# Attention and residual blocks as parts of 8 KB tiles, experts' weights in twenty whole places

## The chip, the cores and the metric

The kernel runs on one core of one Trainium2 chip. The metric is the device time of one execution in microseconds (us). Engines are named as in the profile: PE is TensorE, DVE is VectorE, ACT is ScalarE, POOL is GpSimd, and SP is SyncE, which here issues nearly all DMAs. A tile has 128 partitions; sizes such as 8 KB are bytes of one partition, and 128 rows of 8 KB make 1 MB.

## The reference

```python
def reference(...):
    x = first_block(...)    # two layers: swiglu, three mixer branches (window attention,
                            # gated linear recurrence, attention to 256 memory rows), swiglu
    return second_block(x)  # one hybrid layer

def hybrid_layer(x, ...):   # 256 tokens, width 1024
    h = rms_norm(x, norm1_gain); p = h @ w_in
    y_att  = dilated_window_attention(...) @ w_att_out     # 3 groups x 4 heads
    y_rwkv = rwkv7_time_mix(...)                           # 8 heads
    x = x + (gates[..., :D] * y_att + gates[..., D:] * y_rwkv) @ w_out
    return x + hierarchical_moe(rms_norm(x, norm2_gain), ...)

def expert_block(xb, e):    # 32 experts (4 groups of 8), two of them per token
    hid = silu(xb @ w_expert_gate[e]) * (xb @ w_expert_up[e])    # 1024 -> 512
    return hid @ w_expert_down[e]                                # 512 -> 1024
```

All of it is float32. An expert's three matrices have 6 MB, the 32 experts 192 MB.

## The kernel before, in words

The first block and the hybrid layer's projections stream their weights through a ring of two 1 MB buffers (`raw`, class `Stream`, L121). Each half of a buffer is split by ACT (L126, `wh`) and DVE or POOL (L128, `wl`) into two parts, and PE takes three products (L144 to L146). In the hybrid layer three generators, attention, recurrence and gates, take turns by the string `ORDER`; then `hybrid_out` joins them, `route` picks the experts, and `moe` runs them.

`moe` takes the experts four at a time, in eight rounds. A round reads 24 units of 1 MB: eight of the gate matrices, eight of the up matrices (L1336, output `gu`) and eight of the down matrices (L1359, output `y`). A unit is one expert's share: four blocks k of 128x512. PE goes over the blocks k in the outer loop and over the four experts in the inner one, so that a unit's last block is used just before its group of four is done.

Where a unit is put is a list of places (`Units.at`), filled in turn: unit number i goes into place i mod 19. Places come free while the hybrid layer still runs: `free` adds them as its parts end (`LT`, `scores`, `RB`, `YZ`, `at`, `rw`), and `PACE` says after which of the last streamed weights more units are asked for. Some places are one tile of 8 KB. Others are put together from small tiles, four of 2 KB or two of 4 KB, because attention and the residual stream keep their values in 2 KB tiles: `qk` 6, `hv` 3, `bias` 3, `T` 3 (pools of `AB`) and `x` 6 (`NX`). Such a place is loaded by four DMAs with rows of 2 KB (L1129); POOL writes one element first where the load has to wait for a point in the program (L1113, L1121). The first place is loaded by four DMAs with rows of 2 KB on its second turn too. The last four units of the last round's up matrices, and the last four of its down matrices, are loaded in halves.

The DMAs of a queue start in the order in which SP issues them. A scheduler that runs at build time, with modelled times, sets this order; a DMA waits at SP for its tile's last reader. It also waits for one of eight completion counters, so that the ninth DMA is issued when the first has landed.

The residual stream `x` is written at L182 and L185 into a new `x` tile in each sublayer, in `hybrid_in` into new ones (`x1`), and in `hybrid_out` again (`x2`). After `moe` each engine reads a flag and branches over a block that is only for experts with more than 32 tokens; then the four output DMAs go (L1372).

Of the kernel before, what the change touches and what calls it, by code (L numbers as in the profile page):

```python
# [8 lines left out]
P=128  # L9
# [99 lines left out]
class Stream:  # L109
# [6 lines left out]
    def _load(s):  # L116
        c=s.c; nc=c.nc; i=s.pos
        if i and i%16==0:
            with c.tc.high_priority() if i>16 else ExitStack():
                s.raw=c.ring.tile([P,2048],F32,tag="ring",name="raw")  # L120
                nc.sync.dma_start(out=s.raw,in_=s.dram[i//16])  # L121
        if i%8==0:
            with c.tc.high_priority():
                s.wh=c.wsp.tile([P,1024],F32R,tag="wh",name="wh"); s.wl=c.wsp.tile([P,1024],F32R,tag="wl",name="wl")
                r=s.raw[:,(i%16)*128:(i%16)*128+1024]
                nc.scalar.copy(s.wh,r)  # L126
                e=nc.gpsimd if s.turns and s.turns[i//8%len(s.turns)] else nc.vector
                e.tensor_tensor(s.wl,r,s.wh.bitcast(F32),op=ALU.subtract)  # L128
            if s.reached: s.reached(s.wh)
# [4 lines left out]

W5=[P,512]
def pst(c,tag,name,shape=None): return c.where["p",tag].tile(shape or [P,2,256],F32,tag=tag,name=name,bufs=c.PT[tag])
def blk(c,tag,name,dt=F32,shape=None): return c.where["b",tag].tile(shape or [P,2,256],dt,tag=tag,name=name,bufs=c.BT[tag])
def bc(r,n=2): return r.unsqueeze(1).to_broadcast([P,n,256])
# [358 lines left out]
NX=6; NRING=2; NW=3  # L497

def pools(c,ex):
    tc=c.tc  # L500
    c.where={}; c.BT={}; c.PT={}
    c.kp=ex.enter_context(tc.tile_pool(name="kp",bufs=1))
    c.xp=ex.enter_context(tc.tile_pool(name="xp",bufs=NX))
    c.ring=ex.enter_context(tc.tile_pool(name="ring",bufs=NRING))
    c.dr=ex.enter_context(tc.tile_pool(name="dr",bufs=1,space=bass.MemoryType.DRAM))
# [18 lines left out]

def xblk(c,name="x"): return c.xp.tile([P,2,256],F32,tag="x",name=name)

# [76 lines left out]
ORDER='grrrggagargrgagaaggrgaagararggrrraarrragrragrrrrarrg'; NP=0; T1=(1, 1, 1, 0, 1, 1, 0, 1, 0); T2=(1, 0, 0, 1)  # L603
RB={"rw":20,"hc":1}; AB={"qk":6,"hv":3,"bias":3,"T":3}; HP={"r":3,"a":2}

# [66 lines left out]
def rwkv(c,X,Rb,lw,gu,gu2,ins):  # L672
# [195 lines left out]
    def advance(m):  # L868

        t=WC[m]; ps=pst(c,"r","st",[P,4,64])  # L870
        for i in range(4):
            for j in range(2):
                hf=slice(j*64,j*64+64); nc.tensor.matmul(ps[hf,i,:],t[hf,0,i,:],S[m][hf,i,:],start=True,stop=True)
        s=c.sm.tile([P,8,64],F32,tag="S",name="S",bufs=1)[:,:4]
        v.tensor_tensor(s,S[m],pe[:,m,:].unsqueeze(2).to_broadcast([P,4,64]),op=ALU.mult); v.tensor_tensor(t[:,1],t[:,1],s,op=ALU.add)
        v.tensor_tensor(t[:,1],t[:,1],ps,op=ALU.add)
        S.append(t[:,1])
# [45 lines left out]
def hyb_attention(c,X,Rb,rt,db):  # L923
# [38 lines left out]
    den=c.sm.tile([P,4,2,3],F32,tag="hden",name="hden",bufs=1); rd=c.sm.tile([P,4,2],F32,tag="hrd",name="hrd",bufs=1)  # L962
    oh,ol=[c.xp.tile([P,2,256],F32R,tag="x",name=n) for n in ("oh","ol")]
    yield
# [62 lines left out]
def hybrid_in(c,xs,ins,att,rwk):  # L1027
# [5 lines left out]
    for p in range(4):  # L1033
        t=xblk(c,"x1")
        for i in range(2): v.scalar_tensor_tensor(t[:,i,:],xs[p][:,i,:],gf[:,2*p+i:2*p+i+1],Rf,op0=ALU.mult,op1=ALU.mult)
        x1.append(t)
# [11 lines left out]
def hybrid_out(c,xs):  # L1048
# [13 lines left out]
    for p in range(4):  # L1062
        ps=w[2*p:2*p+2] if p<2 else gemm_last(c,8,M,"wo") if p==3 else gemm_pair(c,8,M,"wo")
        t=xblk(c,"x2"); add_out(c,t,ps,x1[p],None); yield t

MP={"y":2,"a":3}
NRW=5
PACE=[0, 0, 0, 0, 1, 2, 0, 0, 0, 0, 0, 0, 1, 1, 1, 0, 0, 1, 0, 0, 0, 3, 1, 0]
# [19 lines left out]
def moe_consts(c,ins):  # L1088
# [3 lines left out]
    c.mc=c.kp.tile([P,136+CAP],F32,name="mc"); nc.sync.dma_start(out=c.mc,in_=ins['mc'])  # L1092

class Units:

    def __init__(s,c,ex,ins): c.un=s; s.c=c; s.ex=ex; s.ins=ins; s.i=0; s.got=[]; s.two=[]; s.at=[]; s.j=0; s.big=None; s.gap=[]
    def pool(s,name,bufs=1): return s.ex.enter_context(s.c.tc.tile_pool(name=name,bufs=bufs,reuse_waits="tile")),"u"
# [3 lines left out]
    def load(s,after=None):  # L1101

        c=s.c; nc=c.nc; i=s.i; s.i+=1; n=s.j%len(s.at); p=s.at[n]; again=s.j//len(s.at)==1; s.j+=1
        w=s.ins['we'][i//24,i%24//8,i%8//4,i%4]; last=i>=176 and i%8>3; Q=range(0,2048,512)
        back=range(4)[::-1] if n<2 else range(4)
        def tile(x,n):
            b=1 if x[1]=="S" else c.BT.get(x[1])
            return x[0].tile([P,n],F32,tag=x[1],name="unit",**({"bufs":b} if b else {}))
        with c.tc.high_priority():
            if len(p)==1 and not (again and n==0):  # L1110
                r=tile(p[0],2048); q=[r[:,a:a+512] for a in Q]
                if n==0: s.big=q
                if after is not None: nc.gpsimd.tensor_copy(r[:1,:1],after[:1,:1].bitcast(F32))  # L1113
                z=[[(r[:,a],w[:,a])] for a in (slice(0,1024),slice(1024,2048))] if last else [[(r,w)]]
            else:

                if len(p)==1: q=s.big
                elif len(p)==2: q=[t[:,a:a+512] for t in [tile(x,1024) for x in p] for a in (0,512)]
                else: q=[tile(x,512) for x in p]
                if after is not None:  # L1120
                    for t in q: nc.gpsimd.tensor_copy(t[:1,:1],after[:1,:1].bitcast(F32))  # L1121
                z=[[(q[k],w[:,k*512:k*512+512])] for k in back]
            if last:

                s.two.append([sum(z[:len(z)//2],[]),sum(z[len(z)//2:],[])])
                z=[sum(x,[]) for x in zip(*s.two)] if i%4==3 else []
                if i%4==3: s.two=[]
            for x in z:
                for d,src in x: nc.sync.dma_start(out=d,in_=src)  # L1129
        return q  # L1130
# [3 lines left out]
    def free(s,name):  # L1134

        c=s.c; A=lambda t,n: [(c.where["b",t],t)]*n
        if name=="LT": s.more((c.u8,"big"))
        if name=="scores": s.more(*A("qk",4)); s.more(*A("qk",2),*A("bias",2))
        if name in ("RB","YZ"): s.more((c.r8,"u"))
        if name=="at": s.more(*A("hv",3),*A("bias",1)); s.gap.append(0)  # L1140
        if name=="rw":
            s.rest=[s.pool(f"u{i}") for i in range(NRW)]+[s.pool("gap",2)]; s.gap.append(0)
        if len(s.gap)==2:

            g=s.rest.pop(); s.gap=[]
# [124 lines left out]
def moe(c,m,ins,out):  # L1270
    nc=c.nc; v=nc.vector
    q=m.q; G5=m.G5; rt=m.rt; g32=vec(c,'norm2'); io=m.io; acc=m.acc; Hh=m.Hh; Hl=m.Hl; mt=m
    def overflow(acc):
        over=nc.values_load(mt.fi,min_val=0,max_val=1)
        with c.tc.If(over>0):
            x=[t[:,2*i:2*i+2,:] for t in [c.wsp.tile([P,4,256],F32,tag=n,name="ox") for n in ("wh","wl")] for i in range(2)]
            for t in range(2):
                for n in range(2):
                    w=xblk(c,"oh").rearrange("p a b -> p (a b)")
                    for p in range(2): v.tensor_tensor(w[:,p*256:p*256+256],Hh[2*n+p][:,t,:].bitcast(F32),Hl[2*n+p][:,t,:].bitcast(F32),op=ALU.add)  # L1280
# [5 lines left out]
            with c.tc.For_i(0,8,1) as r:  # L1286
                ge=c.sm.tile([P,2,1,4],F32,tag="oge",name="oge",bufs=1)
                nc.sync.dma_start(out=ge,in_=mt.dG[:,:,bass.ds(r,1),:])
                for e in range(4):
# [94 lines left out]
def body(tc,v,ins,out,dbg=None):  # L1384
    with ExitStack() as ex:
# [34 lines left out]
```

## Time and profile before

| | |
|---|---|
| three runs, median | 2137.96 us (2134.9 to 2139.03) |
| the profiled execution, its own time | 2128.82 us |
| its span | 2127.1 us |
| PE busy | 1946.0 us (91%) |
| DVE, ACT, POOL busy | 1139.9, 842.4, 94.0 us |
| first expert matmul `gu` starts | 1654.5 us |
| moved by DMA in all | 475.27 MB |

The span is one execution's from its first to its last instruction; its own time is 1.7 us longer. Instruction counts are the profile's: a float32 matmul stands there twice.

### The profile page before, as it was taken

To read this page: it belongs to the slowest core of one execution; us is meant where nothing else is said; L and a number is where in the kernel's file an instruction comes from. 1 tells how busy PE (TensorE), PEld (TensorE's weight loads), DVE (VectorE), ACT (ScalarE), POOL (GpSimd) and SP (SyncE) were. 2 spreads that over 40 slices of the span, in tenths; PEclk is the share of its full clock that TensorE was granted. 3 is DMA by queue.
4 is the path that set the end of the run, shared out by engine and by line. 5 is a ranking of instruction groups with operands and counts; after the bars stand their busy time and mean duration, and the time that the engine had idled before them with its cause. 6 is when DMAs were issued, how large, how long until landed. Compare 5 with 4: busy or idle time off the path is not lost.

```text
span 2127.1 us, 35735 instructions
## 1 busy us (share of the span) xinstructions
PE 1946.0 (91%) x15063; PEld 1668.7 (78%) x15063; DVE 1139.9 (54%) x1778; ACT 842.4 (40%) x1253; POOL 94.0 (4%) x71
## 2 busy tenths in 40 slices
PE   8999999999999999999998999999998876767665
PEld 8999999999999999999997999898988321212111
DVE  6566786676656566687575656776667210101110
ACT  5454565444444444476544444543534100000000
POOL 0000000000000000000000000444002000000000
PEclk9999999999999999999999999999999898888788
DMA  6565444455555555534457555433549899999997
GB/s 210 181 226 185 162 139 139 171 186 179 178 181 183 188 201 200 180 138 141 159 181 181 179 180 186 166 120 100 184 140 355 333 397 410 398 404 401 395 405 297
DMA packets 109617, 475.27 MB, mean 223 GB/s; under 512 B 17737, under 2 KB 21356, under 8 KB 63372
## 3 DMA queue, kind: packets, MB, share of 16 engines
q1 hardware_dynamic: 96624, 462.07, 59.8%
q10 hardware_dynamic: 12828, 10.87, 2.2%
q8 instruction: 120, 1.97, 0.4%
q14 instruction: 45, 0.37, 0.0%
HBM read 468.93 MB, written 3.96 MB: 222 GB/s over the span
## 4 chain that ended last, share of the span: by engine, by line
PE 73%; DMA 21%; DVE 4%; ACT 1%; issue 0%; SPq 0%; POOL 0%; ACTq 0%; DVEq 0%
DMA unit<-in_we 19%; PE g L144 4%; PE g L145 4%; PE g L146 4%; PE d L145 4%; PE d L144 4%; PE d L146 4%; PE u L146 4%; PE u L144 4%; PE u L145 4%; PE gt L144 3%; PE gt L146 3%; PE gt L145 3%; DMA raw<-in_w 2%; PE br L145 2%; PE br L146 2%
## 5 line engine op out<-in xcount | busy, mean ns | idle before, releaser
L126 ACT CAST wh<-raw 128x1024 fp32r<-128x1024 f32 x491 | 513.8, 1048 | 692.3 <-PE g L145 128.9
L128 DVE TENSOR_TENSOR wl<-raw,wh 128x1024 fp32r<-128x1024 f32 x469 | 575.4, 1227 | 341.8 <-ACT wh L126 338.1
L1336 PE MATMUL gu<-unit,W 128*32 128x512 f32 x1024 | 185.9, 735 | 90.7 <-DMA unit<-in_we 90.7
L144 PE MATMUL g<-xh,wh 128*128 128x256 f32 x768 | 219.1, 286 | 16.9 <-ACT wh L126 16.9
L145 PE MATMUL g<-xl,wh 128*128 128x256 f32 x768 | 219.5, 286 | 0.0
L146 PE MATMUL g<-xh,wl 128*128 128x256 f32 x768 | 216.2, 285 | 0.0
L1336 PEld LDWEIGHTS gu<-unit,W 128*32 128x32 f32 x1024 | 40.2, 127 | 216.1 <-DMA unit<-in_we 147.4
L145 PE MATMUL d<-l,wh 128*128 128x256 f32 x704 | 199.2, 283 | 0.0
L146 PE MATMUL d<-h,wl 128*128 128x256 f32 x704 | 198.8, 283 | 0.0
L144 PE MATMUL d<-h,wh 128*128 128x256 f32 x704 | 197.3, 280 | 0.0
L144 PE MATMUL u<-xh,wh 128*128 128x256 f32 x640 | 181.9, 284 | 2.3 <-ACT wh L126 2.3
L146 PE MATMUL u<-xh,wl 128*128 128x256 f32 x640 | 181.9, 284 | 0.8 <-DVE wl L128 0.8
L145 PE MATMUL u<-xl,wh 128*128 128x256 f32 x640 | 181.7, 284 | 0.0
L144 PEld LDWEIGHTS g<-xh,wh 128*128 128x128 f32 x768 | 149.4, 194 | 17.1 <-ACT wh L126 17.1
L145 PEld LDWEIGHTS g<-xl,wh 128*128 128x128 f32 x768 | 149.4, 195 | 0.1
L146 PEld LDWEIGHTS g<-xh,wl 128*128 128x128 f32 x768 | 147.7, 194 | 0.1
L144 PE MATMUL gt<-xh,wh 128*128 128x256 f32 x512 | 147.0, 287 | 0.0
L146 PE MATMUL gt<-xh,wl 128*128 128x256 f32 x512 | 146.6, 286 | 0.0
L145 PE MATMUL gt<-xl,wh 128*128 128x256 f32 x512 | 146.5, 286 | 0.0
L144 PEld LDWEIGHTS d<-h,wh 128*128 128x128 f32 x704 | 133.9, 190 | 0.0
L146 PEld LDWEIGHTS d<-h,wl 128*128 128x128 f32 x704 | 132.1, 188 | 0.0
L145 PEld LDWEIGHTS d<-l,wh 128*128 128x128 f32 x704 | 131.7, 187 | 0.0
(511 smaller groups left out, 4234.4 us busy)
## 6 DMA issues: line engine op xcount, KB each, us to landing
raw<-in_w SPq DMA_DIRECT2D x245, 1024.0 KB, 4.9
unit<-in_we SPq DMA_DIRECT2D x115, 1024.0 KB, 10.8
unit<-in_we SPq DMA_DIRECT2D x284, 256.0 KB, 7.7
unit<-in_we SPq DMA_DIRECT2D x12, 512.0 KB, 10.0
dbias<-brow ACTq DMA_DIRECT2D x1, 2304.0 KB
mem<-in_mem ACTq DMA_DIRECT2D x8, 256.0 KB, 5.6
bd<-in_bd ACTq DMA_DIRECT2D x8, 256.0 KB, 6.1
bias<-dbias ACTq DMA_DIRECT2D x6, 256.0 KB, 4.9
```

The source lines that it names most:

```text
L126: nc.scalar.copy(s.wh,r)
L128: e.tensor_tensor(s.wl,r,s.wh.bitcast(F32),op=ALU.subtract)
L144: nc.tensor.matmul(ps,wh,XH[k],start=start,stop=False)
L145: nc.tensor.matmul(ps,wh,XL[k],start=False,stop=False)
L146: nc.tensor.matmul(ps,wl,XH[k],start=False,stop=stop)
L1336: nc.tensor.matmul(ps[e*32:e*32+32,:],XT[4*h+k][:,j*128+e*32:j*128+e*32+32],W[e][k],start=(h==0 and k==ks[0]),stop=(h==1 and k==ks[3]),til ...
```

## The change

Four 8 KB tiles `A0` to `A3` take the attention's blocks: `slot` hands out 2 KB parts of them in rotation. `qk` has parts 0 to 5, `bias` 6, 7 and 11, `hv` 8 to 10, `T` 12 to 15. The residual stream has six parts of `xa` (8 KB) and `xb` (4 KB) in rotation; `x1` and `x2` are written over `x`. A new pool `ep` has a place from the start of the hybrid layer on. The reserve for DMA descriptors shrinks to 1024 bytes per partition. There are twenty places: `ep`, `LT`, `A0`, `A1`, two of `r8`, `A2`, `A3`, `u0` to `u5`, `g0`, `g1`, two ring buffers, one pair of `wh` tiles, and `xa`. From unit 20 on each load is ordered behind the load before it.

```diff
+def slot(c,tag,shape=None):
+    f=c.view[tag]; t=f.pop(0); f.append(t)
+    return t if shape==W5 else t.rearrange("p (a b) -> p a b",a=2)
+def parts(t): return [t[:,a:a+512] for a in range(0,t.shape[1],512)]
 def blk(c,tag,name,dt=F32,shape=None):
+    if tag in c.view: return slot(c,tag,shape)
...
-    c.xp=ex.enter_context(tc.tile_pool(name="xp",bufs=NX))
+    c.xp=ex.enter_context(tc.tile_pool(name="xp",bufs=1,reuse_waits="tile"))
+    c.ep=ex.enter_context(tc.tile_pool(name="ep",bufs=1,reuse_waits="tile"))
+    c.view={"x":parts(c.xp.tile([P,2048],F32,tag="xa",name="xa"))+parts(c.xp.tile([P,1024],F32,tag="xb",name="xb"))}
...
-AB={"qk":6,"hv":3,"bias":3,"T":3}
+AB={"A0":1,"A1":1,"A2":1,"A3":1}
...
-        t=xblk(c,"x1")
+        t=xs[p]
...
-        t=xblk(c,"x2"); add_out(c,t,ps,x1[p],None); yield t
+        t=x1[p]; add_out(c,t,ps,t,None); yield t
-NRW=5
+NRW=6
...
+            if again and n==0:
+                q=s.big; z=[[(q[k],w[:,k*512:k*512+512])] for k in range(4)[::-1]]
+            else:
+                if len(p)==1: r=tile(p[0],2048); t=[r[:,a:a+1024] for a in H]; z=[[(r,w)]]
+                else: t=[tile(x,1024) for x in p]; z=None
...
             for x in z:
-                for d,src in x: nc.sync.dma_start(out=d,in_=src)
+                for d,src in x:
+                    k=nc.sync.dma_start(out=d,in_=src).ins
+                    b=s.prev if i>=len(s.at) else c.st.ins if i==0 else None
+                    if b is not None: c.tc.add_manual_dep(k,b.name,INORDER)
+                    s.prev=k
...
-        if name=="scores": s.more(*A("qk",4)); s.more(*A("qk",2),*A("bias",2))
+        if name=="scores": s.more(A("A0")); s.more(A("A1"))
-        if name=="at": s.more(*A("hv",3),*A("bias",1)); s.gap.append(0)
+        if name=="at": s.more(A("A2")); s.gap.append(0)
...
-            for p in s.rest+[(c.u8,"g0"),(c.u8,"g1")]+[(c.ring,"ring")]*NRING: s.add(p)
-            x=(c.xp,"x"); s.add(x,x,x,x); s.add(x,x,g,(c.sm,"S")); s.add(*[(c.wsp,"wh")]*2)
+            for p in [A("A3")]+s.rest+[(c.u8,"g0"),(c.u8,"g1")]+[(c.ring,"ring")]*NRING: s.add(p)
+            s.add(*[(c.wsp,"wh")]*2); s.add((c.xp,"xa"))
...
+        u=Units(c,ex,ins); u.more((c.ep,"u"))
+        A=sum([parts(blk(c,f"A{i}",f"A{i}",F32,[P,2048])) for i in range(4)],[])
+        c.view.update(qk=A[:6],bias=A[6:8]+A[11:12],hv=A[8:11],T=A[12:])
...
-    nc=bacc.Bacc("TRN2",target_bir_lowering=False,num_devices=1)
+    nc=bacc.Bacc("TRN2",target_bir_lowering=False,num_devices=1,dynamic_dma_scratch_size=1024)
```

The order of SP's DMAs changes at three places. The first is the end of the attention part, where places come free between the last streamed weights (`raw`). Before, from the load into `qk` tiles on:

```order
L121 DMA raw_17674<-in_w 128x2048
L1129 DMA unit_17370<-in_we 128x512
L1129 DMA unit_17371<-in_we 128x512
L1129 DMA unit_17380<-in_we 128x512
L1129 DMA unit_17372<-in_we 128x512
L1129 DMA unit_17373<-in_we 128x512
L1129 DMA unit_17378<-in_we 128x512
L1129 DMA unit_17379<-in_we 128x512
L1129 DMA unit_17381<-in_we 128x512
L1129 DMA unit_17632<-in_we 128x512
L1129 DMA unit_17264<-in_we 128x2048
L121 DMA raw_17743<-in_w 128x2048
```

And now, from the same streamed weights to the sixth after them:

```order
L121 DMA raw_17604<-in_w 128x2048
L1138 DMA unit_17321<-in_we 128x2048
L1138 DMA unit_17323<-in_we 128x2048
L1138 DMA unit_17218<-in_we 128x2048
L121 DMA raw_17673<-in_w 128x2048
L1138 DMA unit_17381<-in_we 128x2048
L121 DMA raw_17751<-in_w 128x2048
L1138 DMA unit_17565<-in_we 128x2048
L1138 DMA unit_17679<-in_we 128x2048
L1138 DMA unit_17717<-in_we 128x2048
L121 DMA raw_17822<-in_w 128x2048
```

Ten DMAs, one of them whole, stand between two loads of streamed weights before; now three whole ones stand there, and one of `A2` (17565) ahead of the third.

The second place is the start of the experts, where places are used again. Before, SP's rows there (16566 is the first place, used again in four pieces):

```order
L1129 DMA unit_18451<-in_we 128x512 x2
L1129 DMA unit_16566<-in_we 128x512
L1129 DMA unit_18491<-in_we 128x512
L1129 DMA unit_16566<-in_we 128x512
L1129 DMA unit_18492<-in_we 128x512
L1129 DMA unit_18501<-in_we 128x512
L1129 DMA unit_18493<-in_we 128x512
L1129 DMA unit_18489<-in_we 128x2048
L1129 DMA unit_16566<-in_we 128x512
```

And now (14661 is the first place):

```order
L1138 DMA unit_18353<-in_we 128x1024
L1138 DMA unit_18354<-in_we 128x1024
L1138 DMA unit_14661<-in_we 128x512 x4
L1138 DMA unit_18392<-in_we 128x2048
L1138 DMA unit_18394<-in_we 128x2048
L1138 DMA unit_18396<-in_we 128x2048
L1138 DMA unit_18427<-in_we 128x2048
```

The pieces of several units are mixed before; now four pieces of one unit are followed by whole units in the order of their use.

The third place is SP's last loads. Before, from the last halves of the up matrices (20266 to 20269) on:

```order
L1129 DMA unit_20268<-in_we 128x1024
L1129 DMA unit_20309<-in_we 128x512
L1129 DMA unit_20269<-in_we 128x1024
L1129 DMA unit_20303<-in_we 128x2048
L1129 DMA unit_20305<-in_we 128x2048
L1129 DMA unit_20307<-in_we 128x2048
L1129 DMA unit_20310<-in_we 128x512
L1129 DMA unit_20350<-in_we 128x512 x2
L1129 DMA unit_20269<-in_we 128x1024
L1129 DMA unit_20311<-in_we 128x512
L1129 DMA unit_20312<-in_we 128x512
L1129 DMA unit_20351<-in_we 128x512 x2
```

And now, where 19839 to 19842 are the up matrices' halves, 19876 to 19882 the down matrices' first four units and 19913 to 19916 halves of their last four:

```order
L1138 DMA unit_19842<-in_we 128x1024
L1138 DMA unit_19876<-in_we 128x2048
L1138 DMA unit_19878<-in_we 128x2048
L1138 DMA unit_19880<-in_we 128x2048
L1138 DMA unit_19882<-in_we 128x2048
L1138 DMA unit_19913<-in_we 128x1024
L1138 DMA unit_19914<-in_we 128x1024
L1138 DMA unit_19915<-in_we 128x1024
L1138 DMA unit_19916<-in_we 128x1024
L1138 DMA unit_19913<-in_we 128x1024
```

The last half of the up matrices (20269) stands behind seven DMAs of down matrices before; now the up matrices' halves are all issued ahead of the down matrices. Over the whole program SP issues 174 whole units, 34 halves and 4 pieces now.

## Rows read from the trace of the kernel before

**Rows 1.** The page's second part: 40 slices of 53.2 us, tenths and GB/s
```profile
PE   8999999999999999999998999999998876767665
...
GB/s 210 181 226 185 162 139 139 171 186 179 178 181 183 188 201 200 180 138 141 159 181 181 179 180 186 166 120 100 184 140 355 333 397 410 398 404 401 395 405 297
```
**Rows 2.** Waits of PE from 1655 us on: us in total, times, longest
```profile
PE gu L1336 <- DMA unit<-in_we: 90.7, 44, 7.3
```
**Rows 3.** PE in order of time, 1635 to 1685 us: start, us, instructions
```profile
1654.48 3.64 PE L1336 MATMUL gu<-unit,W 128*32 128x512 f32 x32
...
1659.76 10.53 PE L1336 MATMUL gu<-unit,W 128*32 128x512 f32 x96
```
**Rows 4.** Stretches of 2 us around the first expert matmul (last: clock, DMA share, GB/s)
```profile
1650.00:1652.00 2.00, 2.00 (x11) 2.00 (x11) 0.87 (x5) 0.27 (x1) 0.00 (x0) 0.50 0.03 8
...
1654.00:1656.00 2.00, 2.00 (x21) 0.89 (x23) 0.49 (x2) 0.47 (x1) 0.00 (x0) 1.00 0.00 0
1656.00:1658.00 2.00, 2.00 (x20) 0.39 (x12) 0.00 (x0) 0.00 (x0) 0.00 (x0) 1.00 0.65 209
1658.00:1660.00 2.00, 2.00 (x22) 1.85 (x22) 0.48 (x1) 0.61 (x2) 0.00 (x0) 1.00 0.84 266
1660.00:1662.00 2.00, 2.00 (x24) 0.59 (x19) 0.60 (x4) 1.52 (x2) 0.00 (x0) 1.00 0.86 217
1662.00:1664.00 2.00, 2.00 (x24) 0.61 (x19) 0.00 (x0) 0.00 (x0) 0.00 (x0) 1.00 0.95 296
```
**Rows 5.** DMA view of 1655 to 2110 us: packets, issues with KB each
```profile
DMA packets 53568, 181.68 MB, mean 399 GB/s; under 512 B 6076, under 2 KB 6076, under 8 KB 40362
...
unit<-in_we SPq DMA_DIRECT2D x103, 1024.0 KB, 11.6
unit<-in_we SPq DMA_DIRECT2D x256, 256.0 KB, 8.7
unit<-in_we SPq DMA_DIRECT2D x12, 512.0 KB, 10.0
```
**Rows 6.** DMA view, 10 us from 1830, 2030, 1810, 1900, 1960, 2080 us
```profile
DMA packets 584, 4.25 MB, mean 425 GB/s; under 512 B 65, under 2 KB 65, under 8 KB 65
...
DMA packets 581, 4.25 MB, mean 425 GB/s; under 512 B 63, under 2 KB 63, under 8 KB 63
...
DMA packets 1666, 3.94 MB, mean 394 GB/s; under 512 B 189, under 2 KB 189, under 8 KB 1518
...
DMA packets 1751, 3.98 MB, mean 398 GB/s; under 512 B 196, under 2 KB 196, under 8 KB 1621
...
DMA packets 1444, 3.66 MB, mean 366 GB/s; under 512 B 163, under 2 KB 163, under 8 KB 1275
...
DMA packets 1145, 4.22 MB, mean 422 GB/s; under 512 B 129, under 2 KB 129, under 8 KB 1066
```
**Rows 7.** Stretches of 2 us around the last load's landing
```profile
2108.00:2110.00 2.00, 2.00 (x24) 0.64 (x19) 0.00 (x0) 0.00 (x0) 0.00 (x0) 1.00 0.84 336
2110.00:2112.00 2.00, 2.00 (x26) 0.56 (x19) 0.70 (x1) 0.69 (x1) 0.00 (x0) 1.00 0.09 37
```
**Rows 8.** All engines in order of time, 2095 to 2127 us
```profile
2106.82 7.07 PE L1359 MATMUL y<-unit,W 128*32 128x512 f32 x62 [0.73 <-ACT W L1353]
...
2115.62 0.69 ACT L1361 ACTIVATE yh<-y,gs 128x512 fp32r<-128x512 f32 x1 [4.36 <-PE y L1359]
...
2117.19 0.74 DVE L1362 SCALAR_TENSOR_TENSOR yl<-y,gs,yh 128x512 fp32r<-128x512 f32 x1
...
2119.95 1.92 SPq L1372 DMA_DIRECT2D out<-acc  x4
```
**Rows 9.** Waits of SP's DMA queue from 1280 us on
```profile
SPq L1129 <- DMA unit<-in_we: 290.9, 326, 3.0
...
SPq L1129 <- PE ho L1005: 10.6, 1, 10.6
```
**Rows 10.** Waits of PE from 1240 to 1640 us
```profile
PE hv L954 <- DVE hvt L959: 3.2, 1, 3.2
...
PE br L146 <- DVE wl L128: 0.4, 1, 0.4
```

More of the change, by code (lines that the diff above doesn't have):

```diff
@@ L120, in _load @@
                 s.raw=c.ring.tile([P,2048],F32,tag="ring",name="raw")
-                nc.sync.dma_start(out=s.raw,in_=s.dram[i//16])
+                s.ins=nc.sync.dma_start(out=s.raw,in_=s.dram[i//16]).ins
         if i%8==0:
@@ L135, with blk @@
 W5=[P,512]
+def slot(c,tag,shape=None):
+    f=c.view[tag]; t=f.pop(0); f.append(t)
+    return t if shape==W5 else t.rearrange("p (a b) -> p a b",a=2)
+def parts(t): return [t[:,a:a+512] for a in range(0,t.shape[1],512)]
 def pst(c,tag,name,shape=None): return c.where["p",tag].tile(shape or [P,2,256],F32,tag=tag,name=name,bufs=c.PT[tag])
-def blk(c,tag,name,dt=F32,shape=None): return c.where["b",tag].tile(shape or [P,2,256],dt,tag=tag,name=name,bufs=c.BT[tag])
+def blk(c,tag,name,dt=F32,shape=None):
+    if tag in c.view: return slot(c,tag,shape)
+    return c.where["b",tag].tile(shape or [P,2,256],dt,tag=tag,name=name,bufs=c.BT[tag])
 def bc(r,n=2): return r.unsqueeze(1).to_broadcast([P,n,256])
@@ L523, in blocks, with xblk @@
     for t in BT: c.where["b",t]=b
-def xblk(c,name="x"): return c.xp.tile([P,2,256],F32,tag="x",name=name)
+def xblk(c,name="x",shape=None): return slot(c,"x",shape)
 def layers(c,ins):
@@ L603 @@
 ORDER='grrrggagargrgagaaggrgaagararggrrraarrragrragrrrrarrg'; NP=0; T1=(1, 1, 1, 0, 1, 1, 0, 1, 0); T2=(1, 0, 0, 1)
-RB={"rw":20,"hc":1}; AB={"qk":6,"hv":3,"bias":3,"T":3}; HP={"r":3,"a":2}
+RB={"rw":20,"hc":1}; AB={"A0":1,"A1":1,"A2":1,"A3":1}; HP={"r":3,"a":2}
 def final_scale(c,xs,gf):
@@ L873, in advance @@
                 hf=slice(j*64,j*64+64); nc.tensor.matmul(ps[hf,i,:],t[hf,0,i,:],S[m][hf,i,:],start=True,stop=True)
-        s=c.sm.tile([P,8,64],F32,tag="S",name="S",bufs=1)[:,:4]
+        s=c.sm.tile([P,4,64],F32,tag="S",name="S",bufs=1)
         v.tensor_tensor(s,S[m],pe[:,m,:].unsqueeze(2).to_broadcast([P,4,64]),op=ALU.mult); v.tensor_tensor(t[:,1],t[:,1],s,op=ALU.add)
@@ L962, in hyb_attention @@
     den=c.sm.tile([P,4,2,3],F32,tag="hden",name="hden",bufs=1); rd=c.sm.tile([P,4,2],F32,tag="hrd",name="hrd",bufs=1)
-    oh,ol=[c.xp.tile([P,2,256],F32R,tag="x",name=n) for n in ("oh","ol")]
+    o=c.xp.tile([P,1024],F32R,tag="xb",name="o").rearrange("p (n a b) -> p n a b",n=2,a=2); oh,ol=o[:,0],o[:,1]
     yield
@@ L1092, in moe_consts, with __init__ @@
     c.mc=c.kp.tile([P,136+CAP],F32,name="mc"); nc.sync.dma_start(out=c.mc,in_=ins['mc'])
+INORDER=mybir.DependencyInfo(mybir.DependencyClass.NoSync,mybir.DependencyReason.DATA)
 class Units:
-    def __init__(s,c,ex,ins): c.un=s; s.c=c; s.ex=ex; s.ins=ins; s.i=0; s.got=[]; s.two=[]; s.at=[]; s.j=0; s.big=None; s.gap=[]
+    def __init__(s,c,ex,ins): c.un=s; s.c=c; s.ex=ex; s.ins=ins; s.i=0; s.got=[]; s.two=[]; s.at=[]; s.j=0; s.big=None; s.gap=[]; s.prev=None
     def pool(s,name,bufs=1): return s.ex.enter_context(s.c.tc.tile_pool(name=name,bufs=bufs,reuse_waits="tile")),"u"
@@ L1103, in load @@
         c=s.c; nc=c.nc; i=s.i; s.i+=1; n=s.j%len(s.at); p=s.at[n]; again=s.j//len(s.at)==1; s.j+=1
-        w=s.ins['we'][i//24,i%24//8,i%8//4,i%4]; last=i>=176 and i%8>3; Q=range(0,2048,512)
-        back=range(4)[::-1] if n<2 else range(4)
+        w=s.ins['we'][i//24,i%24//8,i%8//4,i%4]; last=i>=176 and i%8>3; H=(0,1024)
         def tile(x,n):
-            b=1 if x[1]=="S" else c.BT.get(x[1])
+            b=c.BT.get(x[1])
             return x[0].tile([P,n],F32,tag=x[1],name="unit",**({"bufs":b} if b else {}))
         with c.tc.high_priority():
-            if len(p)==1 and not (again and n==0):
-                r=tile(p[0],2048); q=[r[:,a:a+512] for a in Q]
-                if n==0: s.big=q
[L1113 to L1122, printed above, removed]
+            if again and n==0:
[3 more added lines that the diff above has]
+                else: t=[tile(x,1024) for x in p]; z=None
+                if after is not None:
+                    for x in ([r] if z else t): nc.gpsimd.tensor_copy(x[:1,:1],after[:1,:1].bitcast(F32))
+                if z is None or last: z=[[(x,w[:,a:a+1024])] for x,a in zip(t,H)]
+                q=[x[:,a:a+512] for x in t for a in (0,512)]
+                if n==0: s.big=q
             if last:
@@ L1134, in free @@
     def free(s,name):
-        c=s.c; A=lambda t,n: [(c.where["b",t],t)]*n
+        c=s.c; A=lambda t: (c.where["b",t],t)
         if name=="LT": s.more((c.u8,"big"))
-        if name=="scores": s.more(*A("qk",4)); s.more(*A("qk",2),*A("bias",2))
+        if name=="scores": s.more(A("A0")); s.more(A("A1"))
         if name in ("RB","YZ"): s.more((c.r8,"u"))
-        if name=="at": s.more(*A("hv",3),*A("bias",1)); s.gap.append(0)
+        if name=="at": s.more(A("A2")); s.gap.append(0)
         if name=="rw":
-            s.rest=[s.pool(f"u{i}") for i in range(NRW)]+[s.pool("gap",2)]; s.gap.append(0)
+            s.rest=[s.pool(f"u{i}") for i in range(NRW)]; s.gap.append(0)
         if len(s.gap)==2:
-            g=s.rest.pop(); s.gap=[]
-            s.add(*A("T",3),g)
-            for p in s.rest+[(c.u8,"g0"),(c.u8,"g1")]+[(c.ring,"ring")]*NRING: s.add(p)
-            x=(c.xp,"x"); s.add(x,x,x,x); s.add(x,x,g,(c.sm,"S")); s.add(*[(c.wsp,"wh")]*2)
+            s.gap=[]
+            for p in [A("A3")]+s.rest+[(c.u8,"g0"),(c.u8,"g1")]+[(c.ring,"ring")]*NRING: s.add(p)
+            s.add(*[(c.wsp,"wh")]*2); s.add((c.xp,"xa"))
             st=c.st; end=-(-st.dram.shape[0]*16//8)
@@ L1274, in overflow @@
         over=nc.values_load(mt.fi,min_val=0,max_val=1)
+        c.view["x"]=parts(c.xp.tile([P,2048],F32,tag="xa",name="oxa"))
         with c.tc.If(over>0):
@@ L1278, in overflow @@
                 for n in range(2):
-                    w=xblk(c,"oh").rearrange("p a b -> p (a b)")
+                    w=xblk(c,"oh",W5)
                     for p in range(2): v.tensor_tensor(w[:,p*256:p*256+256],Hh[2*n+p][:,t,:].bitcast(F32),Hl[2*n+p][:,t,:].bitcast(F32),op=ALU.add)
@@ L1299, in overflow @@
                     for t in range(2):
-                        g=xblk(c,"og").rearrange("p a b -> p (a b)")
+                        g=xblk(c,"og",W5)
                         nc.scalar.activation(g,gu[0][t],AF.Silu); v.tensor_tensor(g,g,gu[1][t],op=ALU.mult)
@@ L1303, in overflow @@
                         for k in range(4): nc.tensor.transpose(ps[:,k*128:k*128+128],g[:,k*128:k*128+128],c.ident)
-                        hT=xblk(c,"ohTs").rearrange("p a b -> p (a b)"); nc.scalar.copy(hT,ps); hs.append(hT)
+                        hT=xblk(c,"ohTs",W5); nc.scalar.copy(hT,ps); hs.append(hT)
                     y=[[pst(c,"d" if t else "y","oy",[P,512]) for t in range(2)] for n in range(2)]
@@ L1395, in body @@
         phase(c,ex,"h",{},{}); ps=ExitStack(); banks(c,ps,"h",HP)
-        u=Units(c,ex,ins)
+        u=Units(c,ex,ins); u.more((c.ep,"u"))
         c.r8=ex.enter_context(c.tc.tile_pool(name="r8",bufs=2,reuse_waits="tile"))
```

## The prediction

> **What bounds the kernel now.** I read the page's slices first. PE is at nine tenths in 28 of the first 30 slices, while DMA moves 100 to 226 GB/s. In the last ten slices it is the other way round: PE falls to five to eight tenths and DMA moves about 400 GB/s in most of them [rows 1]. So the kernel has two stages. Until about 1640 us PE decides, and from the experts on the loads of their weights decide. The waits of PE say the same: 44 waits and 90.7 us for `unit` ahead of `gu` alone [rows 2]. PE's own need is far less: 96 of the profile's matmuls took 10.53 us, 0.110 us each, when nothing was late [rows 3], and a round has 192 of them, 21 us.
>
> Then I looked for when the loads stop and start. From 1650 to 1652 us 8 GB/s are moved and from 1654 to 1656 us nothing [rows 4]: all 19 places are full, and the next load waits for PE's first expert matmuls (from 1654.48 us on [rows 3]). From 1656 us it runs again, at 209 to 296 GB/s for 8 us [rows 4]; I take 1656.7 us as the start, since 0.65 of the first of these stretches is busy. It ends at about 2110.2 us, where the DMA share goes from 0.84 to 0.09 [rows 7]. That is 453.5 us of loading, and then a tail of 16.9 us to the span's end at 2127.1 us. Every microsecond taken from the 453.5 us or from the tail is taken from the kernel, as long as PE keeps up.
>
> **How fast a row of 2 KB and one of 8 KB goes.** In the stretches from 1830 and 2030 us, nearly all packets are of 8 KB: of 581 there are 518, and the other 63 are under 512 bytes [rows 6]. Sixteen engines for 10 us are 160 us, over 518 packets 0.309 us each; a whole unit (128 packets on 16 engines) is 2.47 us, 425 GB/s. In the three stretches from 1810, 1900 and 1960 us most packets are of 2 KB: 1329 of 2 KB beside 148 of 8 KB, 1425 beside 130, and 1112 beside 169. What 160 us leave after the 8 KB packets is 0.086, 0.084 and 0.097 us for a 2 KB packet, 0.089 in the mean. A quarter unit is then 0.712 us, 368 GB/s. The stretch from 2080 us has mostly halves with rows of 4 KB, and 422 GB/s; a half is 1.24 us by it.
>
> These prices give the whole stage back: 256 quarters are 182.3 us, 103 whole units 254.5, 12 halves 14.9 [rows 5], together 451.7 us of the 453.5. The 1.8 us left over are the slow start.
>
> **The change part by part.** *Whole places.* SP issues 174 whole units, 34 halves and 4 quarters in the new order, against 115, 12 and 284. Ahead of the pause go as many units as there are places: twenty, 19 whole ones and one pair of halves. Left are 155 whole units (383.0 us), 32 halves (39.8) and 4 quarters (2.8): 425.6 us, against 451.7. That is 26.1 us less, 2.5 of them for the twentieth place and the rest for the rows. I take the 8 KB price as it stands in two stretches. For the halves the ends are the 8 KB rate, 0.2 us less in all, and the 2 KB rate, 5.8 us more; the stretch nearest to them says 422 GB/s, so I keep it.
>
> *The start.* The first place is loaded again in quarters, as PE frees them. Places two to four come free whole when PE has done its first 32 matmuls, at 1658.1 us [rows 3]; today's start mixes quarters of several places over the 8 us of [rows 4]. Three whole units then fill 7.4 us, and by that time the next four, whose matmuls start at 1659.76 us, are free. I take 1 us of gain out of the 1.8; if the four later come late, it is 3 us of loss.
>
> *Loads in the order of use.* Today the last half of the up matrices is issued behind seven DMAs of down matrices, so PE gets its last `gu` late and both last `y` run behind it, from 2106.82 us on [rows 8]. In the new order the up matrices are complete eight units, about 20 us, before the last byte. Then `gu` and the first `y` are done before it, and behind it stand some ten of the profile's matmuls (1.1 us; 2.2 at half the clock), and what follows today's last `y` matmul at 2115.5 us: 11.6 us, less the 0.9 us that `yl` waits, since `yh` ends at 2116.3 and `yl` starts at 2117.19 behind the first half's additions. That is a tail of 11.8 to 12.9 us in place of 16.9. I take 4 us of gain; the ends are 0, if something else holds the last `y`, and 5.
>
> The order has a price in principle: a load waits behind every earlier one. SP already waits 326 times, 290.9 us, for one of the eight last loads to land [rows 9]; these waits mean that eight are in flight, and eight whole units are 20 us of work. So a wait of SP of some microseconds is covered in the expert stage.
>
> *The hybrid layer.* Attention's parts and `x` keep their count or have one more (`T` 4 in place of 3), and the vector work is the same. The load into `ep` comes in the first block, where DMA moves less than half of what it can [rows 1]. `x1` over `x` waits for the last reader of `x`, and nobody reads it until the layer's end. The start of `route` and of the experts follows PE, which has waits of 3.2 us at most here [rows 10]; the schedule's small shifts may add or take one such wait, so 0, from 3 less to 3 more. The smaller descriptor reserve only makes room.
>
> The sum is 26.1 + 1 + 4, about 31 us. The profiled execution has 2127.1 us of span and 2128.8 us of its own time; it would come to 2098. The median of the runs shown is 9.1 us above it, so the median should go from 2138 to 2107.
>
> Here the Trainium skill speaks against the change: "DMA: Bandwidth & Descriptors", in its Specifications, gives 512 bytes as the smallest transfer that reaches line rate. By that 2 KB rows lose nothing, and 23.6 of the 26.1 us would not come. The trace does not agree, as 2 KB stretches show 366 to 398 GB/s beside 425 [rows 6]; but a stretch of small rows also has small DMAs and mixed places in it, so I keep the case below.
>
> **The rivals.** *The rate is not the rows'.* The slow stretches could be slow for what they load or when, and the average of 400 GB/s (181.4 MB in 453.5 us) would stay. Then 172 units, 180.4 MB, take 450.9 us; with start and tail the gain is 2.4 + 1 + 4, about 7 us: 2131. For it speaks that the stretch from 1960 us is slower than the one from 1900 us at fewer small packets; against it, that both 8 KB stretches, 200 us apart, give the same 425.
>
> *Whole places starve the loads.* A place is free only after the unit's last block. If PE, at half its clock, falls behind, the loads pause again, as they do from 1650 to 1656.7 us [rows 4], some 7 us each time. Two such pauses leave 17 us of gain: 2121. Against it: at half the clock a round's matmuls are 42 us, against 59 us of loads for 24 units, and twenty places are 49 us of loads.
>
> *The ordered queue starves the hybrid layer; slower.* Six loads of streamed weights stand between the units that come free at the end of attention and recurrence. In the new order a load into `A2` stands ahead of one of them; today SP waits 10.6 us for `ho` at that point [rows 9]. If each of the six waited so long and PE with it, the experts would start 64 us later: 33 us slower, 2171. It decides from 31 us of new waits of PE, 5 us for each load. Against it: the same loads stand behind units today, and PE waited 0.4 us for them [rows 10].
>
> **How the numbers follow.** The forecast has 0.80, its own range 2099 to 2116 (the hybrid layer's 3 us, the halves' 5.8, the start's 3, the tail's 4 do not all go one way). Starved loads have 0.08, the unchanged rate 0.08, the slower case 0.04. The range for 8 in 10 is 2097 to 2124: it takes in the starved loads and leaves the other two out. What a measurement can tell from no change is 0.2%, 4.3 us. The first two cases are faster by far; of the third a half may end within it. So faster has 0.92, the same 0.04, slower 0.04.
>
> **What would show it.** After the change the DMA view of the expert stage should show few packets of 2 KB and 418 to 425 GB/s in stretches of 10 us throughout; about 21 MB of units loaded ahead of 1656 us and the same short pause before it; the last load landing near 2083 us; the last `gu` done some 15 us before the last landing, and 12 to 13 us from there to the end. The forecast is wrong if 8 KB stretches fall to 400 GB/s, if gaps without DMA show up among the experts, or if `gu` first starts later than 1658 us.

## The result and the profile after

The median went from 2136.43 us (4 runs) to 2104.72 us (4 runs, 2103.70 to 2108.11): the result gives their ratio as 0.9873, interval 0.9852 to 0.9894 (the two medians alone divide to 0.985). The forecast was 2107 us. The profiled execution has a span of 2103.2 us and 2105.39 us of its own time. Its span is 23.9 us shorter than before's, against 31 forecast. It is the two stages of before again. First PE and GB/s in the slices of the page of after, the answer to [rows 1]:

```profile
PE   8999999999999999999998999999999787767776
GB/s 212 181 223 181 178 141 127 175 181 181 181 181 181 183 184 226 182 129 150 153 183 183 181 180 183 214 116 81 179 136 276 316 424 424 425 423 424 425 424 314
```

Seven slices of the expert stage now lie between 423 and 425 GB/s; before, the same seven spread from 395 to 410. The DMA view of 1700 to 2060 us, of before and then of after, with the median time from issue to landing at a row's end:

```profile
DMA packets 42990, 144.67 MB, mean 402 GB/s; under 512 B 4905, under 2 KB 4905, under 8 KB 32161
...
unit<-in_we SPq DMA_DIRECT2D x86, 1024.0 KB, 12.2
unit<-in_we SPq DMA_DIRECT2D x210, 256.0 KB, 8.2
```

```profile
DMA packets 22357, 152.48 MB, mean 424 GB/s; under 512 B 2607, under 2 KB 2607, under 8 KB 4912
...
unit<-in_we SPq DMA_DIRECT2D x132, 1024.0 KB, 19.5
unit<-in_we SPq DMA_DIRECT2D x21, 512.0 KB, 17.3
```

172 units (180.4 MB) are left after the pause. At 402 GB/s they take 448.7 us and at 424 GB/s 425.4: the rate alone is worth 23.3 us. Now the stretches of 2 us at the start and at the end of the loads in after (last: clock, DMA share, GB/s), which answer to [rows 4, 7]:

```profile
1654.00:1656.00 2.00, 2.00 (x12) 1.57 (x15) 0.78 (x2) 0.47 (x1) 0.00 (x0) 0.56 0.00 0
1656.00:1658.00 2.00, 2.00 (x24) 0.60 (x20) 0.18 (x1) 0.00 (x0) 0.00 (x0) 1.00 0.11 20
1658.00:1660.00 2.00, 2.00 (x21) 0.89 (x11) 0.00 (x0) 0.00 (x0) 0.00 (x0) 1.00 0.72 253
1660.00:1662.00 2.00, 2.00 (x22) 1.34 (x24) 0.97 (x5) 1.15 (x3) 0.00 (x0) 1.00 1.03 224
1662.00:1664.00 2.00, 2.00 (x24) 0.57 (x19) 0.12 (x1) 0.98 (x1) 0.00 (x0) 1.00 0.79 250
1664.00:1666.00 2.00, 2.00 (x24) 0.65 (x19) 0.00 (x0) 0.00 (x0) 0.00 (x0) 1.00 0.96 403
2084.00:2086.00 2.00, 1.77 (x12) 0.29 (x10) 0.72 (x1) 0.69 (x1) 0.00 (x0) 1.00 0.97 391
2086.00:2088.00 2.00, 2.00 (x12) 0.52 (x4) 0.03 (x1) 0.00 (x0) 0.00 (x0) 1.00 0.62 246
2088.00:2090.00 2.00, 2.00 (x8) 0.49 (x8) 0.17 (x1) 0.00 (x0) 0.00 (x0) 1.00 0.24 98
2090.00:2092.00 2.00, 2.00 (x14) 0.53 (x14) 1.11 (x2) 0.00 (x0) 0.00 (x0) 1.00 0.01 4
```

The loads run from 1657.8 us (0.11 of the stretch from 1656 is busy) to about 2089.1, if the busy shares of the last stretches are added up: 431.3 us in place of 453.5. The tail is then 14.1 us in place of 16.9. The end is soft, though: single packets still come after 2090 us, and the last one ends at 2090.35 (in before at 2111.0). Counted from there the tail is 12.9 us in place of 16.1. The first `gu` starts at 1655.59 us, 1.1 us later. So the span's 23.9 us are 22.2 from the loads and 2.8 from the tail, less 1.1; with the last packet as the loads' end they are 21.8 and 3.2. The end of after in order of time, which answers to [rows 8]:

```profile
2070.98 1.90 PE L1349 MATMUL gu<-unit,W 128*32 128x512 f32 x10 [0.22 <-DMA unit<-in_we]
...
2089.28 0.73 PE L1379 MATMUL po<-yl,OTs 128*128 128x512 f32 x2
...
2089.95 2.68 PE L1372 MATMUL y<-unit,W 128*32 128x512 f32 x14
...
2092.73 0.69 ACT L1374 ACTIVATE yh<-y,gs 128x512 fp32r<-128x512 f32 x1 [7.48 <-PE y L1372]
2093.45 0.75 DVE L1375 SCALAR_TENSOR_TENSOR yl<-y,gs,yh 128x512 fp32r<-128x512 f32 x1 [2.33 <-ACT yh L1374]
...
2096.22 1.92 SPq L1385 DMA_DIRECT2D out<-acc  x4
```

The last `gu` ends at 2072.9 us, 16 us before 2089.1. PE's last `y` ends at 2092.63: 3.5 us behind 2089.1, and 2.3 us behind the last packet. PE's waits from 1655 us on, the answer to [rows 2]:

```profile
PE gu L1349 <- DMA unit<-in_we: 67.7, 51, 3.8
PE y L1372 <- DMA unit<-in_we: 23.4, 22, 2.7
```

PE still waits for loads, but 23 us less for `gu`. The bound is the same, and it runs faster.

### The profile page after: what moved, and what is told of

It reads as the page before. It is cut to its first block, busy times and chain, and to the rows that moved or that the text cites. A ratio compares the mean times of both kernels' runs of the same rounds, so it can differ in the third digit from the quotient of the medians.

```text
span 2103.2 us, 35407 instructions
## 1 busy us (share of the span) xinstructions
PE 1951.3 (93%) x15063; PEld 1670.8 (79%) x15063; DVE 1139.4 (54%) x1778; ACT 842.1 (40%) x1253; POOL 93.0 (4%) x68
## 4 chain that ended last, share of the span: by engine, by line
PE 74%; DMA 20%; DVE 4%; ACT 1%; issue 1%; POOL 0%; SPq 0%; ACTq 0%; DVEq 0%; POOLq 0%
DMA unit<-in_we 17%; PE g L151 4%; PE g L152 4%; PE g L153 4%; PE d L152 4%; PE d L153 4%; PE d L151 4%; PE u L153 4%; PE u L151 4%; PE u L152 4%; PE gt L151 3%; PE gt L153 3%; PE gt L152 3%; DMA raw<-in_w 2%; PE br L152 2%; PE br L153 2%
## 5 line engine op out<-in xcount | busy, mean ns | idle before, releaser
L1349 PE MATMUL gu<-unit,W 128*32 128x512 f32 x1024 | 198.4, 677 | 67.7 <-DMA unit<-in_we 67.7
L1349 PEld LDWEIGHTS gu<-unit,W 128*32 128x32 f32 x1024 | 44.8, 121 | 198.8 <-DMA unit<-in_we 125.6
```

What stands on the lines that cost most here:

```text
L1349: nc.tensor.matmul(ps[e*32:e*32+32,:],XT[4*h+k][:,j*128+e*32:j*128+e*32+32],W[e][k],start=(h==0 and k==ks[0]),stop=(h==1 and k==ks[3]),til ...
```

## The experiments

All edits are to the changed kernel, and all but four in the line that goes through a unit's DMAs. Lengths of the loads are those of one profiled execution each. Two theories stand against each other. By the first a load is slow for its 2 KB rows. By the second it is slow for something that came along with them: the DMA's size, the mixture of places, or the order.

**All loads as quarters, 2 KB rows.**
```
-for d,src in x:
+for d,src in [(d[:,a:a+512],src[:,a:a+512]) for d,src in x for a in range(0,d.shape[-1],512)]:
```


> The changed kernel (2104.7 us) with every expert load cut into DMAs with rows of 2 KB into the same whole places, in the same order. If the length of a row sets the rate, 180 MB go at 368 to 398 GB/s in place of 424: the expert stage's loads take 453 to 490 us in place of 432, 2125 to 2165 us in all, and 10 us stretches show 360 to 398 GB/s throughout. If the slow stretches of the kernel before came from what was loaded or from the mixed places, it stays at 2105 us and 424 GB/s.

Measured: 2145.42 us, 1.0062 of before (1.0042 to 1.0083). DMA view of 1700 to 2060 us:

```profile
DMA packets 76825, 139.84 MB, mean 388 GB/s; under 512 B 8663, under 2 KB 8663, under 8 KB 76809
...
unit<-in_we SPq DMA_DIRECT2D x532, 256.0 KB, 5.3
```

The loads take 468.0 us. With the order and the places of after kept, the quarters alone undo the whole gain and more. But 388 GB/s are 0.676 us a quarter, less than the 0.712 of the forecast, and a quarter has small rows and is a small DMA at once.

**256 KB again, but 8 KB rows: 32 neighbouring partitions each.**
```
+for d,src in [(d[a:a+32],src[a:a+32]) for d,src in x for a in range(0,128,32)]:
```


> The changed kernel with every expert load cut into four DMAs of 32 partitions, rows of 8 KB as they were (4 KB for the halves): as many bytes per DMA as in the kernel before. If the length of a row sets the rate, 424 GB/s stay and the time is 2101 to 2109 us; the last 4 us before the last landing, in which the rate falls to 98 GB/s, get shorter if they come from 8 MB in flight, since now only 2 MB are. If the size of a DMA (or eight small ones in flight) sets the rate, it falls to 368 to 398 GB/s as in the kernel with 2 KB rows: 2125 to 2165 us.

Measured: 2515.19 us, 1.1794 (1.1768 to 1.1819). The same view:

```profile
DMA packets 15648, 80.02 MB, mean 222 GB/s; under 512 B 5304, under 2 KB 5304, under 8 KB 6346
## 3 DMA queue, kind: packets, MB, share of 16 engines
q1 hardware_dynamic: 15638, 79.88, 101.2%
```

Half the rate, with engines that count as busy throughout. Neither theory expected it: which partitions a DMA spans, and with them which rows of the source, came in as a third quantity, so the run says nothing on rows.

**The same with every fourth partition.**
```
+for d,src in [(d[a::g],src[a::g]) for d,src in x for g in [4 if d.shape[-1]==2048 else 1] for a in range(g)]:
```


> The changed kernel with every whole unit cut into four DMAs of every fourth partition: 32 rows of 8 KB and 256 KB each, as in the kernel with 32 neighbouring partitions (226 GB/s, 2515 us), but spread over all 128. If that one was slow because all sixteen engines write to the same 32 partitions at a time, 415 to 425 GB/s are back and the time is 2101 to 2112 us; then neither the size of a DMA nor the bytes in flight set the rate, and the end of the loads should fall off sharply. If 32 rows or 256 KB per DMA are slow by themselves, it stays near 226 GB/s, or at 390 GB/s as with 2 KB rows.

Measured: 2138.69 us, 1.0036 (1.0018 to 1.0055), 396 GB/s. SP's waits between 1700 and 2060 us, here and then in the run with 2 KB quarters:

```profile
SPq L1138 <- DMA unit<-in_we: 18.9, 25, 1.6
```

```profile
SPq L1138 <- DMA unit<-in_we: 159.8, 513, 0.9
```

```profile
1743.54 21.56 SPq L1138 DMA_DIRECT2D unit<-in_we  x34
```

The third row is of the timeline of this run. SP hardly waits for landings any more: 34 DMAs in 21.56 us, 0.634 us each with 1.9 us of waits among them, and 256 KB per 0.634 us are 413 GB/s. From 1700 to 2060 us its 529 DMAs take 0.62 us each when all its waits (32.5 us) are left out; the 533 of the run with 2 KB quarters take 0.37. So it is issuing these DMAs that got slower. Where SP has to wait for PE it can't catch up: the stretches from 1745 and 1748 us have DMA shares of 0.92 and 0.83. SP's own issuing is thus the likely bound here. That is argued, not shown: over the whole stretch the engines still count as busy for 99.6% of the time. The run doesn't decide about rows either.

**512 KB a DMA, once with 2 KB rows, once with 8 KB rows.** With half as many DMAs SP waits for landings in both (174.9 and 212.1 us of the 360).
```
 2 KB: two pieces of 512 columns out of each row, in each of two DMAs
+tuple(t.rearrange("p (a b n) -> p b a n",a=2,b=2)[:,y] for t in (d,src)) ... for y in range(2)
 8 KB: every second partition
+for d,src in [(d[a::g],src[a::g]) for d,src in x for g in [2 if d.shape[-1]==2048 else 1] for a in range(g)]:
```


> The changed kernel with every whole unit loaded by two DMAs of 512 KB whose rows are two pieces of 2 KB (blocks 0 and 2, then 1 and 3): rows as short as in the kernel with 2 KB quarters (389 GB/s, 2145 us), but twice the bytes per DMA and 4 MB in flight. If the length of a row sets the rate, 385 to 392 GB/s and 2138 to 2148 us. If the size of a DMA or the bytes in flight set it, nearer to 424 GB/s: 2105 to 2125 us.

> The changed kernel with every whole unit cut into two DMAs of every second partition: 64 rows of 8 KB, 512 KB. With one DMA per unit the stage runs at 423 GB/s (2.48 us a unit), with four of 8 KB rows at 396 (2.65 us). If each DMA has a fixed cost on every engine, some 0.056 us by these two, a unit takes 2.54 us with two: 414 GB/s and 2113 to 2117 us. If what was slow with four was that few rows fall to an engine, two rows of a DMA, it is near 423 GB/s: 2103 to 2109 us.

Measured: 2133.53 us with 2 KB rows, 1.0016 (0.9999 to 1.0034), and 2106.59 us with 8 KB rows, 0.9886 (0.986 to 0.9913). The view of 1700 to 2060 us, 2 KB rows first:

```profile
DMA packets 72686, 143.50 MB, mean 399 GB/s; under 512 B 4516, under 2 KB 4516, under 8 KB 72672
...
unit<-in_we SPq DMA_DIRECT2D x273, 512.0 KB, 10.5
```

```profile
DMA packets 24512, 152.27 MB, mean 423 GB/s; under 512 B 4785, under 2 KB 4785, under 8 KB 7098
...
unit<-in_we SPq DMA_DIRECT2D x290, 512.0 KB, 9.9
```

This pair decides. The size of a DMA, the places, the order and the number of DMAs are the same; the rows are four times as long, and the rate is 6% higher. A DMA with 8 KB rows also covers only every second partition, but that costs nothing: 512 KB go as fast as the 1024 KB over all partitions did (423 against 424). So a fixed price of a DMA plays no part from 512 KB on, and the rows do. With 2 KB rows 399 lies between the two expectations: from 256 to 512 KB they gain 11 GB/s (388 to 399), whose cause no run separates.

The packets in the traces say where the rows' price lies. Between 1700 and 2060 us a packet of 2 KB takes 84 ns in the median, one of 4 KB about 160 and one of 8 KB 309; the 84 and 309 are the same in before and in the mixture below. So four packets of 2 KB are 336 ns where one of 8 KB is 309: by this estimate each packet costs some 9 ns beside its bytes.

**Seven of the twenty places in quarters, as a mixture.**
```
+... for g in [512 if n in (2,3,6,7,10,18,19) and not last else d.shape[-1]] for a in range(0,d.shape[-1],g)]:
```


> The changed kernel with seven of its twenty places loaded in quarters with rows of 2 KB (65 units in quarters, 71 in the kernel before), whole tiles and the order of use kept. If the kernel before lost by its rows alone, a quarter costs what it costs with 2 KB rows throughout (0.674 us from 389 GB/s), 0.23 us more per unit: 15 us, 2117 to 2123 us. If mixing small and large DMAs costs by itself, the quarter costs 0.712 us as in the kernel before: 24 us, 2126 to 2132 us.

Measured: 2119.39 us, 0.9955 (0.9938 to 0.9972). The view of 1700 to 2060 us:

```profile
DMA packets 41398, 146.39 MB, mean 407 GB/s; under 512 B 4728, under 2 KB 4728, under 8 KB 29816
...
unit<-in_we SPq DMA_DIRECT2D x91, 1024.0 KB, 10.4
unit<-in_we SPq DMA_DIRECT2D x195, 256.0 KB, 8.9
```

Nearly the mixture of before (86 and 210), in the new order and places. The loads take 447.9 us, 16.6 more than in after: most of the 22.2 us, put back by the quarters alone. But this execution (2124.28 us) is the longest of ten; by the medians the mixture puts back 14.7 us.

**Without the written order.**
```
-b=s.prev if i>=len(s.at) else c.st.ins if i==0 else None
+b=c.st.ins if i==0 else None
```


> The changed kernel without the ordering of loads from unit 20 on (the first unit keeps its place behind the last weights asked for). The build then swaps neighbours within groups of four, and the last 28 loads stay in the same order. If whole places are what puts the loads in the order of use, 2103 to 2107 us and a tail of 13 us; if the ordering is what shortens the tail, 16 to 17 us of tail and 2108 to 2110 us.

Measured: 2107.28 us, 0.9899 (0.9865 to 0.9934); loads of 430.7 us at 424 GB/s, a tail of 14.6. Nothing that can be told from after.

**The last up matrices late, as before.**
```
+if i==183 and g==1: s.ahead(4)
```


> The changed kernel with the last halves of the up matrices loaded behind the down matrices' first four units, as far from the end (4.2 MB) as in the kernel before; nothing else is moved. If the order of the last loads gave the shorter tail, the last gu comes about 10 us before the last landing and the tail from the last landing to the end goes from 13.3 to 16 or 17 us: 2108 to 2109 us. If the tail is set by something else, it stays at 13.3 us and 2105 us.

Measured: 2107.15 us, 0.9874 (0.985 to 0.9899). The median does not separate it from after; the trace does: the tail is 15.9 us in place of 14.1. Its last `gu` and `y`:

```profile
2076.65 5.67 PE L1350 MATMUL gu<-unit,W 128*32 128x512 f32 x16 [7.95 <-DMA unit<-in_we]
...
2084.62 6.21 PE L1373 MATMUL y<-unit,W 128*32 128x512 f32 x54 [0.73 <-ACT W L1367]
```

PE stands for 7.95 us with down matrices at hand and has 54 `y` to do at the end. The order of the last eight units is worth 1.3 to 1.8 us: without the written order, which leaves the last loads as they are, the tail is 14.6 us.

**Nineteen and twenty-one places.**
```
-NRW=6
+NRW=5                                  (nineteen)
+s.add(s.pool("gap"),(c.xp,"xb"))       (twenty-one; S and S0 move to the recurrence's pool)
```


> The changed kernel with one place less (NRW 5, 19 places). If the stage is loads from the pause to the end, one more unit is loaded behind the pause: the loads end 2.5 us later, 2107 us. If the twentieth place is loaded in time that the loads would have had anyway, or the pause shrinks for another reason, it stays within 0.5 us of 2105 us in the trace's landing of the last load.

> The changed kernel with a twenty-first place: the 4 KB of xb and a new tile of 4 KB, made room for by moving two recurrence tiles (S, S0) into the pool that closes with the recurrence. If a place ahead of the pause is worth one unit of loading, the loads end 2.5 us earlier than with twenty places, 2102.2 us; the step from 19 to 20 places measured 1.2 us in the trace, which would make it 2103.5 us. If the loads then fill the pause too late, or the pair's two DMAs cost what the place brings, 2105 us or more.

Measured: 2107.56 us with nineteen, 0.9884 (0.9865 to 0.9904), loads of 432.5 us: 1.2 more, where 2.5 or less than 0.5 was expected. With twenty-one 2110.69 us, 0.9899 (0.9878 to 0.992): loads of 428.8 us, 2.5 less, as long as one unit takes; but in its profiled execution (2114.66 us, the longest of six) the first `gu` comes at 1667.0 us, 11.4 later. The time is lost in the hybrid layer. The stretch from 1360 to 1380 us, of twenty-one places and then of after:

```profile
1360.00:1380.00 20.00, 18.05 (x87) 13.12 (x87) 14.09 (x20) 9.63 (x18) 4.13 (x2) 0.74 0.31 106
```

```profile
1360.00:1380.00 20.00, 19.30 (x105) 13.32 (x104) 11.84 (x25) 15.75 (x30) 4.73 (x2) 1.00 0.35 118
```

Here the granted clock is 0.74 against 1.00, and PE does 87 matmuls against 105. The moved `S` shifts the work there; whether the clock or the shifted work came first was not tried. A place more doesn't pay in this form.

**Halves of 64 neighbouring partitions.**
```
+for d,src in [(d[a:a+g],src[a:a+g]) for d,src in x for g in [64 if d.shape[-1]==2048 else 128] for a in range(0,128,g)]:
```


> The changed kernel with every whole unit cut into two DMAs of 64 neighbouring partitions, rows of 8 KB. With 32 neighbouring partitions per DMA the stage ran at 226 GB/s, with 32 spread ones at 396. If what a DMA's partitions span limits the rate, 64 neighbours allow twice the 226 GB/s and the count of DMAs decides: about 414 GB/s and 2110 to 2120 us. If neighbouring partitions collide in any case, the rate is well below 396 GB/s and the time above 2140 us.

Measured (one round): 2417.26 us, 1.1341 (1.1297 to 1.1385). The view of 1700 to 2060 us:

```profile
DMA packets 15279, 95.96 MB, mean 267 GB/s; under 512 B 3066, under 2 KB 3066, under 8 KB 4090
...
unit<-in_we SPq DMA_DIRECT2D x184, 512.0 KB, 15.6
```

Beside 423 GB/s for the same bytes, size and row length over every second partition, what is left is which partitions a DMA spans, and with them which rows of the source it reads. No run separates these two.

## Why the prediction was right, and what was mis-sized

**The rate of the loads** carried the forecast, and it held: 424 GB/s throughout, from 8 KB rows. The rival by which the rate would stay is refuted by after, and its reason by the pair of 512 KB. There the rule of the Trainium skill that the forecast weighed ("DMA: Bandwidth & Descriptors", Specifications: 512 bytes reach line rate) does not agree with the runs: 2 KB rows stay at 399 where 8 KB rows reach 423.

Its size was too large. The forecast had 26.1 us and 1 us for the start; measured are 22.2, so 4.9 are missing:
- The start: from 1657.8 to 1664 us 1.49 MB are moved, which at 424 GB/s is 3.5 of 6.2 us. 2.7 us are lost where the forecast left 0.8. Before loses as much by the same reckoning: 1.98 MB in the 7.3 us from 1656.7 to 1664 us [rows 4], 2.6 us more than at 424 GB/s. So the start gained nothing; the forecast had put its loss in before at the 1.8 us that its prices left over, which was too little.
- The end: from 2084 us on 1.47 MB take 5.1 us, 3.5 at the full rate. 1.6 us are lost, in the stretches at 246 and 98 GB/s. Before had a much sharper end [rows 7]; the run with quarters too. The 512 KB run ends as softly as after, so fewer bytes in flight alone do not mend it; what does was not found.
- The remaining 1.4 us are about the difference between 425 and 424 GB/s.

The price of 0.712 us per quarter was too high as a price of the quarter. All quarters gave 0.676, and the mixture 0.617 + 16.6/232 = 0.689 (from 1655 us on it has 236 quarters, after has 4). With the price of the first run the 256 quarters of before would explain 256 x 0.059 = 15 us, with the second 18 (less by the medians). So of some 20 us that remain beside the place, 2 to 5 or somewhat more belong to what else differs in before: its mixture within units, its places, its pauses of single stretches, such as the 366 GB/s of 1960 us [rows 6]. The packets narrow it down. The median packet of 2 KB is no dearer in before (84 ns), but the mean is 88.5 ns against 86.9 with all quarters, and that of an 8 KB packet is 315 against 311 in after. So some packets take longer in before; what holds them up stays open.

**The twentieth place** had 2.5 us. Taking it away cost 1.2 us in the trace, adding another gave 2.5 in the length of the loads.

**The tail** had 4 us and brought 2.8, or 3.2 from the last packet on; the 12.9 us that it then has are the upper end of the forecast's 11.8 to 12.9. What was mis-sized is PE's work behind the last landing: 2.3 us from the last packet on, 3.5 from 2089.1, in place of the 1.1 that the forecast had at the full clock (1.00 is granted from 2090 to 2092 us). Two `po` of the first half and fourteen `y` stand there in PE's order, not ten `y`. From the last `y` on the end is 10.6 us, as worked out (11.6 less 0.9). That the order of the last units is the larger part of the cause is shown by the run with late up matrices, at 1.3 to 1.8 us. **The order elsewhere** was costed at nothing, and without it nothing changed.

**The hybrid layer** had 0, within 3, and brought 1.1 us of loss. That is within what executions differ by: without the written order and with 512 KB of 8 KB rows, edits that leave this layer's own work alone, the first `gu` comes at 1654.02 and 1654.75 us. SP's wait that the slower rival built on is one of 10.8 us for `ht`, as the 10.6 for `ho` before [rows 9], and PE's longest wait there is 3.8 us (3.2 before [rows 10]); the rival is refuted. So is the one by which whole places starve the loads: the pause before 1656 us is there again, but from 1700 to 2060 us no slice of 9 us is below 413 GB/s.

The median came out 2.3 us below the forecast although the gain in the trace was 7 us short of it: the profiled execution of before was 7.6 us below its median (2128.8 against 2136.4), that of after only 0.7 above its own. The forecast carried the 9.1 us over to after; they weren't there. So the mechanism was right, the gain in the trace came a quarter short, and that the median still came so close is luck. In the later series before has medians of 2130 to 2134 us; the ratio of 0.9873 is 27 us of these.

## What to carry to other kernels

Where loads decide, make the piece of memory that comes free as long per partition as the row of a load, rather than several short ones: at equal size of the DMA, 8 KB rows moved 6% more than 2 KB rows. Price such a change by stretches of one kind alone, not by stretches in which sizes and rows are mixed, and take the loss at the start and at the end of the loading as terms of their own. Before a DMA is split further, look at who waits: once SP no longer waits for landings, its own issuing may be the bound.

## What the runs showed of the hardware beyond that

DMAs of 8 KB rows over 32 or 64 neighbouring partitions ran at 222 and 267 GB/s between 1700 and 2060 us, while the sixteen engines counted as 101 and 102% busy; over every fourth or second partition the same bytes ran at 396 and 423. So a full DMA share does not mean a full rate: a packet of 8 KB took 601 and 501 ns there in the median, against 309 ns in after. With views of every fourth partition SP took 0.62 us per DMA without its waits, with quarters of all 128 partitions 0.37.
